# The mLSTM stage of a hybrid decoder step: its small work cut into five phases per pair of heads, and placed between the dense units by a written order

## The chip, the cores and the metric

The kernel runs on one core of one Trainium2 chip. Its time is the device time of one execution in microseconds (us). The core has five engines that each work through their own queue in order: TensorE (PE, matmuls; PEld is its loading of weights), VectorE (DVE), ScalarE (ACT), GpSimd (POOL), and SyncE (SP), which here only issues DMAs.

## The reference

One inference step of a two-layer trunk, on 512 prompt columns and 32 sample columns (8 sequences of 4). Layer 1's mixer, the mLSTM, is the part that changes:

```python
proj = xn @ w_in
qk_raw, v, o_pre, if_pre = jnp.split(proj, [...], axis=-1)
qk = conv_b + sum(conv_w[j] * xpad[:, j:j + T] for j in range(4))     # causal convolution
q, k = jnp.split(jax.nn.silu(qk), 2, axis=-1)                         # 8 heads of 64
o = jax.nn.sigmoid(o_pre)
def chunk_step(carry, inp):
    C, n, m = carry
    ...
    S = jnp.einsum('bhtk,bhsk->bhts', q_c, k_c) * Dw
    num = w_inter[..., None] * jnp.einsum('bhvk,bhtk->bhtv', C, q_c) + jnp.einsum('bhts,bhsv->bhtv', S, v_c)
    den = w_inter * jnp.einsum('bhk,bhtk->bht', n, q_c) + S.sum(-1)
    h = num / jnp.maximum(jnp.abs(den), jnp.exp(-m_t))[..., None]
    C = w_state[..., None, None] * C + jnp.einsum('bhs,bhsv,bhsk->bhvk', w_s, v_c, k_c)
    ...
h = h * lax.rsqrt(jnp.mean(h * h, -1, keepdims=True) + NORM_EPS) * norm_w
out = (h * o) @ w_out
```

## The kernel before

Activations lie with features on the 128 partitions and the 544 columns (512 prompt, 32 sample) along the free axis. `PARTS` cuts the columns into 256 and 288. Every dense product is fp32 made of three fp32r matmuls (`mm3`: high by high, high by low, low by high), so each weight tile that a DMA on SP brings (`wr`) is first split, ACT writing the high half (`wh`, in `split`) and DVE the low half (`wl`). A dense product of 8 blocks over one part is 24 matmuls into one PSUM bank (tag `ps`); with two banks in this stage, the third such unit may begin when DVE has read the first one out.

The stage (`mlstm`) first projects gates and values (`mlstm_inputs`), then in the scope `ml2`: 16 units of 24 matmuls for q and k (`mlstm_qk`, four pairs of heads j, each with a q block and a k block; DVE multiplies each part by the norm factor into `raw`, and then does the causal convolution in nine steps), 16 units of 24 for the output gates (`mlstm_gate`, tag `og`), and 32 units of 12 for the output projection (`project_out`, two halves of four heads, DVE adding each into `x`): 384 matmuls each. After it follows the feed-forward `f1b`.

The small work of a pair is fp32 matmuls of at most 129 columns. `mlstm_weights` loads two rows by DMA and spreads them over the partitions (`qi` from `dwi`, `d` from `dc`), makes the decay weights `d` on DVE and ACT, and multiplies them by k times q (L1376, L1381). `mlstm_pair` then goes chunk by chunk (z = 0 to 3 of 128 columns, z = 4 the samples): transpose k (L1404) and scale it on ACT into `kt`, weights times values (L1413), `qi` times the state (L1415), copy to `hx` and sum of squares on ACT, the next state (L1445 and DVE's L1448, L1450); for the samples also L1426, and L1438 with DVE's update of `cn`. `mlstm_heads` normalises `hx` (ACT's square root, DVE's L1475) and transposes it back (L1479). `mlstm_out` multiplies by the gate and splits for the output projection.

What stands in which order is decided by the Tile scheduler, from the order in the program and its own estimate of times; `high_priority(MOFF)` draws the small work ahead of program order:

```python
for j in range(4):
    if j < 3:
        self.mlstm_qk(j + 1, xs, rs)
    with self.tc.high_priority(MOFF):
        if j < 3:
            self.mlstm_weights(j + 1)
        self.mlstm_pair(j)
        self.mlstm_heads(j)
```

Of the kernel before, what the change touches and what calls it, by code (L numbers as in the profile page):

```python
# [13 lines left out]
ALU = mybir.AluOpType  # L14
# [17 lines left out]
NOG = 6  # L32
# [3 lines left out]
MOFF = 1000  # L36
# [205 lines left out]

class Trunk:
# [255 lines left out]
    def project_out(self, name, xs, halves=1):  # L499

        n = KT // halves
        for ks in (range(h * n, (h + 1) * n) for h in range(halves)):
            xk = [xs(k) for k in ks]
            for m in range(KT):
                def evac(i, hs, ps, m=m):
                    self.V.tensor_tensor(self.x[m][:, hs], ps, self.x[m][:, hs], op=ALU.add)
                self.dense(self.a[name][m][:, ks.start * P:ks.stop * P], xk, evac)
# [641 lines left out]
    def mlstm(self):  # L1149
        with self.scope("ml", nps=0):  # L1150
# [11 lines left out]
            with self.scope("ml2", nps=2):  # L1162
                self.wS, self.hx = {}, {}
                self.mlstm_qk(0, xs, rs)
                with self.tc.high_priority(MOFF):
                    self.mlstm_weights(0)
                for j in range(4):
                    if j < 3:
                        self.mlstm_qk(j + 1, xs, rs)
                    with self.tc.high_priority(MOFF):  # L1170
                        if j < 3:
                            self.mlstm_weights(j + 1)
                        self.mlstm_pair(j)
                        self.mlstm_heads(j)
                ogs = [self.mlstm_gate(h, xs, rs) for h in range(NOG)]
                ys = [self.mlstm_out(h, ogs[h]) for h in range(8 - NOG)]
                ogs += [self.mlstm_gate(h, xs, rs) for h in range(NOG, 8)]
                self.project_out("m_out", lambda h: ys[h] if h < len(ys) else self.mlstm_out(h, ogs[h]), 2)

    def mlstm_inputs(self, xs, rs):  # L1180
# [29 lines left out]
        for g in range(2):  # L1210
# [12 lines left out]
            if g == 0:  # L1223
# [78 lines left out]
    def mlstm_qk(self, j, xs, rs):  # L1302

        V, S, seq, cvo = self.V, self.S, self.by_seq, self.cvo
        cv0v = self.cv0.rearrange("p (k b t) -> p k b t", k=8, t=3)
        for mt in (j, 4 + j):
            raw = self.unit("raw", 2)

            def evac(i, hs, ps, raw=raw):
                V.tensor_tensor(raw[:, hs], ps, rs[i], op=ALU.mult)  # L1310
            self.dense(self.a["m_qk"][mt], xs, evac)
# [13 lines left out]
            (self.q if mt < 4 else self.k)[j] = acc  # L1325
        if j == 3:
            self.nc.sync.dma_start(self.o["o_conv"], cvo)

    def mlstm_gate(self, h, xs, rs):
        t = self.rp("og", NOG, [P, TT])  # L1330

        def evac(i, hs, ps):
            self.V.tensor_tensor(t[:, hs], ps, rs[i], op=ALU.mult)
        self.dense(self.a["m_o"][h], xs, evac)
        self.S.activation(t, t, AF.Tanh, scale=0.5)
        self.V.tensor_scalar(t, t, 0.5, 0.5, op0=ALU.mult, op1=ALU.add)
        return t
# [8 lines left out]
    def mlstm_weights(self, j):  # L1346
# [5 lines left out]
        pS_ = lambda: self.bank("pS", 2)  # L1352
# [4 lines left out]
        wl = self.local("wl_", 2, [P, 4])  # L1357
# [159 lines left out]
```

## Time and profile before

| | |
|---|---|
| median of 3 runs | 2579.95 us (2577.47 to 2580.44) |
| the profiled execution | 2580.45 us |
| its span, first to last instruction | 2578.7 us |
| mean granted clock of TensorE | 0.966 |
| the mLSTM stage from its first q/k matmul to the first matmul of `f1b` | 1913.6 to 2163.4 us of the span |

Times in the views are us from the span's start. An fp32 matmul stands in the trace as two PE instructions, an fp32r one as one. A granted clock of 1.00 is 2.4 GHz, 0.50 is 1.2 GHz; a mean between them is a stretch that had both. "Idle before" an instruction is how long its engine had nothing, and the arrow names what ended that. Some matmul records are missing from the trace, a few per cent.

### The profile page before, as it was taken

Reading aid. Unit: us, or ns where it says so; the run is one execution under the profiler, and the core shown is the slowest. Engines: PE = TensorE matmul, PEld = TensorE weight load, DVE = VectorE, ACT = ScalarE, POOL = GpSimd, SP = SyncE. Lnnn points to the kernel's source line nnn. Section 1 sums busy time; section 2 is a strip of 40 time slices with the busy share of each in tenths; the row PEclk is TensorE's granted clock in tenths of the full one; section 3 lists DMA queues with packets and bytes.
Section 4 is the critical chain, followed back from the end, with each engine's and each line's share of the span. In section 5 each row is a group of like instructions: output and inputs, shape, how many; then the busy total and the mean of one; then the engine's idle time right before and its main releaser. Section 6 shows DMA issues by size and latency. Waiting matters only on the chain.

```text
span 2578.7 us, 54194 instructions
## 1 busy us (share of the span) xinstructions
PE 2476.4 (96%) x21731; PEld 2323.5 (90%) x21731; DVE 1583.1 (61%) x3178; ACT 1258.1 (49%) x2772; POOL 497.6 (19%) x514
## 2 busy tenths in 40 slices
PE   9998999999889999998999999999998999999997
PEld 8998988888778788897999999999977879999997
DVE  6668787777897786665666544433536546444433
ACT  6555666665666564564555433332435435333322
POOL 1204333233431342330110011110000000111100
PEclk9999999999789899998999999999998979999999
DMA  7564543324233233453555432233242212223232
GB/s 218 182 195 143 159 125 113 113 90 137 80 97 111 86 98 116 120 163 116 163 166 167 121 95 85 84 92 91 81 113 80 65 56 91 90 83 94 84 90 72
DMA packets 102220, 291.63 MB, mean 113 GB/s; under 512 B 12569, under 2 KB 28345, under 8 KB 101969
## 3 DMA queue, kind: packets, MB, share of 16 engines
q1 hardware_dynamic: 101968, 288.18, 36.8%
q8 instruction: 170, 2.79, 0.4%
q14 instruction: 82, 0.66, 0.1%
HBM read 278.76 MB, written 9.38 MB: 112 GB/s over the span
## 4 chain that ended last, share of the span: by engine, by line
PE 85%; DVE 9%; issue 2%; ACT 2%; DMA 1%; POOL 1%; SPq 0%; DVEq 0%; ACTq 0%; POOLq 0%
PE ps L346 17%; PE ps L348 17%; PE ps L347 17%; PE pd L346 7%; PE pd L347 7%; PE pd L348 7%; DVE wl L343 2%; DVE m L668 1%; PE ps L1220 1%; PE ps L1221 1%; PE ps L1222 1%; PE b L912 1%; PE ps L1110 1%; PE pc L1034 1%; DVE mx L670 1%
## 5 line engine op out<-in xcount | busy, mean ns | idle before, releaser
L343 DVE TENSOR_TENSOR wl<-wr,wh 128x512 fp32r<-128x512 f32 (+2 forms) x1025 | 723.8, 708 | 480.4 <-ACT wh L342 450.1
L342 ACT CAST wh<-wr 128x512 fp32r<-128x512 f32 (+2 forms) x1025 | 621.8, 609 | 672.8 <-PE ps L347 433.2
L346 PE MATMUL ps<-a,wh 128*128 128x288 f32 (+1 forms) x2384 | 698.5, 293 | 12.3 <-ACT a L394 5.1
L348 PE MATMUL ps<-a,wl 128*128 128x288 f32 (+1 forms) x2384 | 694.3, 291 | 0.2 <-DVE wl L343 0.2
L347 PE MATMUL ps<-a,wh 128*128 128x288 f32 (+1 forms) x2384 | 688.4, 289 | 0.3
L346 PEld LDWEIGHTS ps<-a,wh 128*128 128x128 f32 x2384 | 453.0, 190 | 16.3 <-ACT a L394 5.6
L347 PEld LDWEIGHTS ps<-a,wh 128*128 128x128 f32 x2384 | 453.0, 190 | 2.3 <-DVE a L395 1.1
L348 PEld LDWEIGHTS ps<-a,wl 128*128 128x128 f32 x2384 | 450.7, 189 | 1.4 <-DVE wl L343 0.4
L418 POOL TENSOR_TENSOR t<-t,t 128x256 f32<-128x256 f32 (+1 forms) x132 | 141.6, 1073 | 858.0 <-ACT wh L342 409.9
L346 PE MATMUL ps<-h,wh 128*128 128x288 f32 (+1 forms) x1056 | 303.9, 288 | 0.0
L347 PE MATMUL ps<-h,wh 128*128 128x288 f32 (+1 forms) x1056 | 303.4, 287 | 0.0
L348 PE MATMUL ps<-h,wl 128*128 128x288 f32 (+1 forms) x1056 | 303.2, 287 | 0.0
L346 PE MATMUL pd<-rk,wh 128*128 128x288 f32 (+1 forms) x656 | 198.2, 303 | 6.4 <-DVE t L478 2.7
L347 PE MATMUL pd<-rk,wh 128*128 128x288 f32 (+1 forms) x656 | 197.9, 302 | 1.1 <-DVE rk L395 1.1
L348 PEld LDWEIGHTS ps<-h,wl 128*128 128x128 f32 x1056 | 198.9, 188 | 0.0
L347 PEld LDWEIGHTS ps<-h,wh 128*128 128x128 f32 x1056 | 198.9, 188 | 0.0
L346 PEld LDWEIGHTS ps<-h,wh 128*128 128x128 f32 x1056 | 198.6, 188 | 0.0
L348 PE MATMUL pd<-rk,wl 128*128 128x288 f32 (+1 forms) x656 | 196.7, 300 | 0.0
L342 ACT CAST h<-t 128x256 fp32r<-128x256 f32 (+1 forms) x132 | 55.3, 419 | 198.4 <-POOL t L418 198.4
L347 PE MATMUL pd<-mx,wh 128*128 128x256 f32 (+1 forms) x448 | 135.5, 304 | 9.5 <-DVE mx L670 6.6
L346 PE MATMUL pd<-mx,wh 128*128 128x256 f32 (+1 forms) x448 | 134.0, 302 | 4.2 <-ACT rk L691 1.9
L346 PEld LDWEIGHTS pd<-rk,wh 128*128 128x128 f32 x656 | 127.2, 194 | 10.0 <-ACT mx L669 2.9
(451 smaller groups left out, 4586.2 us busy)
## 6 DMA issues: line engine op xcount, KB each, us to landing
wr<-in_f0a_u_dram SPq DMA_DIRECT2D x44, 512.0 KB, 3.7
wr<-in_f0b_g_dram SPq DMA_DIRECT2D x44, 512.0 KB, 3.6
wr<-in_f0b_u_dram SPq DMA_DIRECT2D x44, 512.0 KB, 3.5
wr<-in_f0a_g_dram SPq DMA_DIRECT2D x43, 512.0 KB, 3.6
wr<-in_f0b_d_dram SPq DMA_DIRECT2D x24, 512.0 KB, 3.7
wr<-in_f1a_g_dram SPq DMA_DIRECT2D x22, 512.0 KB, 4.7
wr<-in_f1a_u_dram SPq DMA_DIRECT2D x22, 512.0 KB, 3.5
wr<-in_f1b_g_dram SPq DMA_DIRECT2D x22, 512.0 KB, 3.6
```

Source lines behind the costliest of these rows:

```text
L342: self.S.copy(dst_h, src)
L343: self.V.tensor_tensor(dst_l, src, dst_h, op=ALU.subtract)
L346: self.T.matmul(out, wh, xh, start=start, stop=False)
L347: self.T.matmul(out, wh, xl, start=False, stop=False)
L348: self.T.matmul(out, wl, xh, start=False, stop=stop)
L418: self.G.tensor_tensor(s, s, w, op=ALU.mult)
L668: V.scalar_tensor_tensor(m, d, self.vec("mu", c * 8 + k), xn, op0=ALU.mult, op1=ALU.add)
L670: (self.G if k % 2 else V).tensor_tensor(l, m, h.bitcast(F32), op=ALU.subtract)
L912: T.matmul(pg[:, (1 - h) * 512 + i * P:(1 - h) * 512 + (i + 1) * P], flat(xc[R[h], i]), flat(arc[R[h], i]), start=True, stop=True)
L1034: T.matmul(py[R[h], out(a)], uv[:, a, c, h, :], gm[:, a, c, 1 - h, 64:128], start=True, stop=st is None)
L1110: T.matmul(pn[R[h], :], xt[H, h * 64:(h + 1) * 64], um, start=True, stop=True)
L1220: T.matmul(pss[q][:n, :], xs[k][0][:, ts], wt(cs)[0], start=k == 0, stop=False)
```

## The change

`dense`'s products of the stage become lists of units (one part of one block each: `dense_units`, `project_units`), in one list `todo`: the q and k blocks of pairs 1 to 3, the gates, then the output projection. Pair 0's q and k run ahead of it. The small work of a pair becomes five phases over all chunks (`mlstm_weights`, `mlstm_states`, `mlstm_values`, `mlstm_sample`, `mlstm_heads`), twenty in all, in one list `small`. A loop walks through `todo` and calls the next phase each time another twentieth of the cost written for the first 44 units (2 for each of 28, 1 for each of 16) is done; the last phases so fall among the units of the output projection's first half. No priority is set any more, and the scheduler orders the rest.

Inside the phases: k is transposed four chunks to a bank and scaled into `kt` by one DVE operation (before: two on ACT for each chunk); all states come before all values; `hx` is copied three chunks at a time and its squares are read from SBUF; the scaling of `hx` is one DVE operation for all chunks and both heads (before: ten); the transposed gate columns `cols` are copied at once. `qi` becomes one full tile of 128 partitions for each head, with the other head's half set to zero by POOL, and L1415's product over 64 rows becomes one over 128 (L1494). The PSUM banks `pS`, `px` and `po` (two each) become six of `sm`. `d` has four buffers in place of six, `qi` four (two pairs) in place of three (three pairs), `og` five in place of six.

```diff
-NOG = 6
+NOG = 5
...
+    def sm(self):
+        return self.bank("sm", 6)
...
+    def dense_units(self, ap, xs, evac):
+
+        wt = []
+
+        def unit(i, hs):
+            if not wt:
+                wt.append(self.weight(ap))
+            ps = self.ps()[:, :hs.stop - hs.start]
+            n = ap.shape[-1] // P
+            for k in range(n):
+                x = xs[k]
+                self.mm3(ps, *wt[0](slice(k * P, (k + 1) * P)), x[0][:, hs], x[1][:, hs], k == 0, k == n - 1)
+            evac(i, hs, ps)
+        return [lambda i=i, hs=hs: unit(i, hs) for i, hs in enumerate(PARTS)]
+
+    def project_units(self, name, ys, half):
+
+        units = []
+        for m in range(KT):
+            def evac(i, hs, ps, m=m):
+                self.V.tensor_tensor(self.x[m][:, hs], ps, self.x[m][:, hs], op=ALU.add)
+            ks = slice(half * 4 * P, (half + 1) * 4 * P)
+            units += self.dense_units(self.a[name][m][:, ks], Shift(ys, half * 4), evac)
+        return units
...
-                self.mlstm_qk(0, xs, rs)
-                with self.tc.high_priority(MOFF):
-                    self.mlstm_weights(0)
+                for u in self.mlstm_qk(0, xs, rs):
+                    u()
+
+                ogs, ys = {}, {}
+                todo = [u for j in range(1, 4) for u in self.mlstm_qk(j, xs, rs)]
+                for h in range(8):
+                    todo += self.mlstm_gate(h, xs, rs, ogs)
+                for half in range(2):
+                    todo += self.project_units("m_out", ys, half)
+                cost = [2] * 28 + [1] * 32
+                small = []
                 for j in range(4):
-                    if j < 3:
-                        self.mlstm_qk(j + 1, xs, rs)
-                    with self.tc.high_priority(MOFF):
-                        if j < 3:
-                            self.mlstm_weights(j + 1)
-                        self.mlstm_pair(j)
-                        self.mlstm_heads(j)
-                ogs = [self.mlstm_gate(h, xs, rs) for h in range(NOG)]
-                ys = [self.mlstm_out(h, ogs[h]) for h in range(8 - NOG)]
-                ogs += [self.mlstm_gate(h, xs, rs) for h in range(NOG, 8)]
-                self.project_out("m_out", lambda h: ys[h] if h < len(ys) else self.mlstm_out(h, ogs[h]), 2)
+                    small += [lambda j=j: self.mlstm_weights(j), lambda j=j: self.mlstm_states(j),
+                              lambda j=j: self.mlstm_values(j), lambda j=j: self.mlstm_sample(j),
+                              lambda j=j: self.mlstm_heads(j)]
+                done, per = 0, sum(cost[:44]) / len(small)
+                for i, u in enumerate(todo):
+                    while small and done >= per * (20 - len(small)):
+                        small.pop(0)()
+                    for h in range(8):
+                        if h in self.hn and h in ogs and h not in ys:
+                            ys[h] = self.mlstm_out(h, ogs[h])
+                    u()
+                    done += cost[i]
...
-        qi = self.unit("qi", 3)
-        for h in range(2):
-            nc.sync.dma_start(qi[R[h]], self.rows["wi"][2 * j + h:2 * j + h + 1, :].to_broadcast([64, TT]))
+
+        qi = [self.unit("qi", 4) for _ in range(2)]
         wl = self.local("wl_", 2, [P, 4])
-        S.copy(wl, qi[:, MLC - 1:TP:MLC])
-        V.tensor_tensor(qi, q, qi, op=ALU.mult)
-
-        wS = [self.unit("d", 6) for _ in range(2)]
+        for h in range(2):
+            self.G.memset(qi[h][R[1 - h]], 0.0)
+            nc.sync.dma_start(qi[h][R[h]], self.rows["wi"][2 * j + h:2 * j + h + 1, :].to_broadcast([64, TT]))
+            S.copy(wl[R[h]], qi[h][R[h], MLC - 1:TP:MLC])
+            V.tensor_tensor(qi[h][R[h]], q[R[h]], qi[h][R[h]], op=ALU.mult)
+
+        wS = [self.unit("d", 4) for _ in range(2)]
         for h, d in enumerate(wS):
             hd = 2 * j + h
             nc.sync.dma_start(d, self.rows["c"][hd:hd + 1, :].to_broadcast([P, TT]))
@@ -1369,95 +1416,129 @@
                                    self.csmask[0:TS], op0=ALU.add, op1=ALU.add)
             S.activation(d[:, :TP], d[:, :TP], AF.Exp)
             S.activation(d[0:TS, TP:], d[0:TS, TP:], AF.Exp)
-        pS = [pS_() for _ in range(2)]
+
+        kt = self.local("kt", 2, [P, 5, P])
+        px, pe = self.sm(), self.sm()
+        for z in range(4):
+            T.transpose(px[:, z * P:(z + 1) * P], k[:, z * MLC:(z + 1) * MLC], self.ident)
+        T.transpose(pe[:TS, :P], k[:, TP:], self.ident)
+        for p, zs, n in ((px, slice(0, 4), P), (pe[:, :P], slice(4, 5), TS)):
+            nz = zs.stop - zs.start
+            V.tensor_tensor(kt[:n, zs].rearrange("p z (h d) -> p z h d", h=2), p[:n].rearrange("p (z h d) -> p z h d", z=nz, h=2),
+                            cols[:n, zs, 8 + 2 * j:10 + 2 * j].unsqueeze(3).to_broadcast([n, nz, 2, 64]), op=ALU.mult)
+        pS = [self.sm() for _ in range(2)]
         for z in range(4):
             ts = slice(z * MLC, (z + 1) * MLC)
             for h in range(2):
                 T.matmul(pS[h][:, ts], k[R[h], ts], q[R[h], ts], start=True, stop=True)
+        pe = [self.sm() for _ in range(2)]
+        for h in range(2):
+            T.matmul(pe[h][:TS, :TS], k[R[h], TP:], q[R[h], TP:], start=True, stop=True)
         for h, d in enumerate(wS):
             V.tensor_tensor(d[:, :TP], d[:, :TP], pS[h], op=ALU.mult)
-        pS = [pS_() for _ in range(2)]
-        for h in range(2):
-            T.matmul(pS[h][:TS, :TS], k[R[h], TP:], q[R[h], TP:], start=True, stop=True)
-        for h, d in enumerate(wS):
-            V.tensor_tensor(d[0:TS, TP:], d[0:TS, TP:], pS[h][0:TS, :TS], op=ALU.mult)
-        self.wS[j] = wS, qi, wl
-
+            V.tensor_tensor(d[0:TS, TP:], d[0:TS, TP:], pe[h][0:TS, :TS], op=ALU.mult)
+        self.wS[j] = wS, qi, wl, kt
...
-    def mlstm_pair(self, j):
...
-        for z in range(5):
-            pk = px()
-            T.transpose(pk[:n, :P], k[:, ts], self.ident)
-                S.activation(kt[:n, h * 64:(h + 1) * 64], pk[:n, h * 64:(h + 1) * 64], AF.Copy, scale=cols[:n, z, 8 + hd:9 + hd])
-                po = po_()
-                T.matmul(po[:n, :129], wS[h][:n, ts], vt, start=True, stop=z == 0)
-                if z in (1, 2, 3):
-                    T.matmul(po[:n, :129], qi[R[h], ts], st[R[h], :], start=False, stop=True)
-                S.copy(hx[:n, z, h, :], po[:n, :129])
...
+    def mlstm_states(self, j):
...
+        pn = [self.sm() for _ in range(2)]
+        sts = []
+        for z in range(4):
+            p = pn[z // 3][:, z % 3 * 129:z % 3 * 129 + 129]
+            for h in range(2):
+                hd = 2 * j + h
+                T.matmul(p[R[h]], kt[:, z, h * 64:(h + 1) * 64], self.v1[z][hd // 4][:, hd % 4, :], start=True, stop=True)
+        for z in range(4):
+            p = pn[z // 3][:, z % 3 * 129:z % 3 * 129 + 129]
+            st = self.local("st", 5, [P, 129])
+            if z == 0:
+                V.tensor_copy(st, p)
+            else:
+                V.scalar_tensor_tensor(st, sts[-1], wl[:, z:z + 1], p, op0=ALU.mult, op1=ALU.add)
+            sts.append(st)
...
+    def mlstm_values(self, j):
...
+        pa, pb = [self.sm() for _ in range(2)], [self.sm() for _ in range(2)]
+        at = lambda h, z, n=P: (pa[h] if z < 3 else pb[h])[:n, z % 3 * 129:z % 3 * 129 + 129]
+        for h in range(2):
+            hd = 2 * j + h
+            for z in range(4):
+                ts = slice(z * MLC, (z + 1) * MLC)
+                T.matmul(at(h, z), wS[h][:, ts], self.v1[z][hd // 4][:, hd % 4, :], start=True, stop=z == 0)
+                if z:
+                    T.matmul(at(h, z), qi[h][:, ts], st[z - 1], start=False, stop=True)
...
+            S.copy(hx[:, 0:3, h, :], pa[h][:, :387].rearrange("p (z v) -> p z v", z=3))
+            S.copy(hx[:, 3, h, :], at(h, 3))
+            S.copy(hx[:TS, 4, h, :], at(h, 4, TS))
...
+                S.activation(sq[:n], hx[:n, z, h, :128], AF.Square, accum_out=sc[:n, z, h:h + 1])
...
+    def mlstm_sample(self, j):
...
     def mlstm_heads(self, j):
...
+        V.tensor_tensor(hx[:, :, :, :128], hx[:, :, :, :128], s(4).unsqueeze(3).to_broadcast([P, 5, 2, 128]), op=ALU.mult)
...
-                V.tensor_scalar(hx[:n, z, h, :128], hx[:n, z, h, :128], sc[:n, z, 8 + h:9 + h], None, op0=ALU.mult)
```

PE, pair 3 in the program before: its values (`po`) with the weights `d_26996` and `d_26997`, the state `st`, and the sample products `km`, with no dense product among them.

```order
L1413 MATMUL po_27237<-v_4407_25391,d_26996 128x129
L1413 MATMUL po_27242<-v_4407_25391,d_26997 128x129
L1413 MATMUL po_27257<-v_4409_25393,d_26996 128x129
L1415 MATMUL po_27257<-st_27250,qi_26990 128x129
L1413 MATMUL po_27263<-v_4409_25393,d_26997 128x129
L1415 MATMUL po_27263<-st_27250,qi_26990 128x129
L1438 MATMUL pS_27342<-v_4415_25399,km_27340 128x129
L1413 MATMUL po_27279<-v_4411_25395,d_26996 128x129
```

PE, pair 3 in the changed program: the same products (L1492 and L1494, into `sm`), between units of the output projection (`ps`, L356 to L358).

```order
L356 MATMUL ps_27737<-hi_27220,wh_27733 128x256
L357 MATMUL ps_27737<-k_27221,wh_27733 128x256
L358 MATMUL ps_27737<-hi_27220,wl_27734 128x256
L1494 MATMUL sm_27817<-st_27722,qi_27593 128x129
L1492 MATMUL sm_27817<-v_4411_25395,d_27604 128x129
L1494 MATMUL sm_27817<-st_27724,qi_27593 128x129
L1494 MATMUL sm_27819<-st_27726,qi_27593 128x129
L1492 MATMUL sm_27818<-v_4407_25391,d_27605 128x129
L356 MATMUL ps_27751<-hi_26879,wh_27733 128x288
```

Before, about 40 small products of pair 3 stood behind one another; now a unit of 12 dense matmuls stands between every few of them. In pairs 1 and 2 the phases are not cut: the 24 products of `mlstm_values` stand together there, with units of 24 ahead and behind.

DVE in the program before, while pair 0's sample states (`cn`) and norm factors (`sc`) are made: the decay weights of pair 3 (`d_26996`, `d_26997`) stand among them.

```order
L1463 TENSOR_TENSOR sc_26246<-sc_26246,cols_25388 128x5x2
L1367 SCALAR_TENSOR_TENSOR d_26996<-d_26996,cols_25388,c_c_ml_25211 128x128 x2
L1464 RECIPROCAL sc_26246<-sc_26246 128x5x2
L1367 SCALAR_TENSOR_TENSOR d_26996<-d_26996,cols_25388,c_c_ml_25211 128x128
L1439 SCALAR_TENSOR_TENSOR cn_26374<-cn_26374,ws_25841,pS_26390 128x129
L1367 SCALAR_TENSOR_TENSOR d_26996<-d_26996,cols_25388,c_c_ml_25211 128x128
L1368 SCALAR_TENSOR_TENSOR d_26996<-d_26996,cols_25388,c_c_ml_25211 32x32
```

DVE in the changed program, at the same work of pair 0: here it is the decay weights of pair 2 (`d_27084`, `d_27085`), and the read-out of a q/k unit (`raw_26438`) stands behind them.

```order
L1534 SCALAR_TENSOR_TENSOR cn_26231<-cn_26231,ws_25831,sm_26381 128x129 x3
L1414 SCALAR_TENSOR_TENSOR d_27084<-d_27084,cols_25388,c_c_ml_25211 128x128
L1534 SCALAR_TENSOR_TENSOR cn_26231<-cn_26231,ws_25831,sm_26382 128x129
L1414 SCALAR_TENSOR_TENSOR d_27084<-d_27084,cols_25388,c_c_ml_25211 128x128 x3
L1415 SCALAR_TENSOR_TENSOR d_27084<-d_27084,cols_25388,c_c_ml_25211 32x32
L1534 SCALAR_TENSOR_TENSOR cn_26238<-cn_26238,ws_25831,sm_26387 128x129 x3
L1414 SCALAR_TENSOR_TENSOR d_27085<-d_27085,cols_25388,c_c_ml_25211 128x128
L1534 SCALAR_TENSOR_TENSOR cn_26238<-cn_26238,ws_25831,sm_26388 128x129
L1414 SCALAR_TENSOR_TENSOR d_27085<-d_27085,cols_25388,c_c_ml_25211 128x128
L1368 TENSOR_SCALAR q_26364<-q_26364 128x544
L1414 SCALAR_TENSOR_TENSOR d_27085<-d_27085,cols_25388,c_c_ml_25211 128x128 x2
```

With four buffers of `d`, pair 2 takes pair 0's, so the DMA that fills them can start only behind pair 0's values; before, with six, that held for pair 3 alone.

## Rows read from the trace of the kernel before

**Rows 1.** The page's head: span, and the engines' busy time, share of it and instructions.
```profile
span 2578.7 us, 54194 instructions
PE 2476.4 (96%) x21731; PEld 2323.5 (90%) x21731; DVE 1583.1 (61%) x3178; ACT 1258.1 (49%) x2772; POOL 497.6 (19%) x514
```

**Rows 2.** Stretches: length, busy us (instructions) of each engine, granted clock, DMA share, GB/s.
```profile
1940.00:1950.00 10.00, 10.00 (x87) 9.75 (x87) 10.00 (x27) 6.45 (x18) 0.00 (x0) 1.00 0.31 107
1690.00:1755.00 65.00, 65.00 (x520) 65.00 (x519) 23.91 (x44) 19.71 (x38) 4.31 (x5) 1.00 0.31 89
1913.60:1923.00 9.40, 7.79 (x48) 7.56 (x48) 2.78 (x12) 0.94 (x3) 0.00 (x0) 0.82 0.89 229
1923.00:1977.00 54.00, 53.18 (x408) 48.42 (x409) 37.75 (x106) 29.91 (x98) 2.03 (x2) 0.97 0.35 102
1977.00:1998.00 21.00, 12.09 (x51) 9.74 (x50) 14.67 (x57) 12.09 (x31) 0.00 (x0) 0.55 0.24 78
1998.00:2083.00 85.00, 84.22 (x625) 73.90 (x624) 46.60 (x125) 42.82 (x127) 4.63 (x4) 0.99 0.21 63
2083.00:2112.50 29.50, 27.51 (x104) 18.47 (x104) 12.33 (x48) 10.35 (x47) 2.49 (x2) 0.53 0.18 56
2112.50:2163.40 50.90, 49.80 (x383) 49.33 (x382) 37.10 (x77) 22.07 (x46) 0.00 (x0) 0.97 0.28 89
1913.60:2163.40 249.80, 234.59 (x1612) 207.43 (x1612) 151.24 (x420) 118.17 (x350) 9.16 (x8) 0.88 0.28 83
```

**Rows 3.** The chain, 1957 to 2040: start us, us, what (x instructions).
```profile
1957.29 1.09 PE pS L1376 x16
...
1961.61 0.17 PE pS L1381 x2
...
1965.64 0.37 PE pS L1445 x4
...
1968.18 0.42 PE po L1415 x4
...
1970.46 0.42 PE po L1413 x2
1970.88 0.42 PE po L1415 x2
1971.30 0.37 PE px L1404 x2
...
1972.30 0.64 PE pS L1438 x4
...
1974.95 4.28 DMA d<-dc
...
2023.76 1.00 PE po L1426 x8
...
2039.03 0.44 PE po L1479 x4
```

**Rows 4.** PE in order of time, 1980 to 1999, with its waits.
```profile
1980.51 1.47 PE L1438 MATMUL pS<-v,km 32*128 32x129 f32 x4 [2.18 <-DVE cn L1439]
1985.57 1.33 PE L1479 MATMUL po<-c_c_all,hx 128*128 128x128 f32 x5 [3.60 <-DVE hx L1475]
...
1993.54 0.58 PE L346 MATMUL ps<-a,wh 128*128 128x256 f32 x1 [1.77 <-DVE raw L1310]
...
1998.19 0.41 PE L346 MATMUL ps<-a,wh 128*128 128x256 f32 x1
```

**Rows 5.** The chain in the tail of pair 3, 2083 to 2112.
```profile
2095.60 0.73 PE po L1413 x2
...
2109.00 2.04 DVE hx L1475 x10
```

**Rows 6.** DVE in order of time, with its waits.
```profile
1979.25 0.61 DVE L1367 SCALAR_TENSOR_TENSOR d<-d,cols,c_c_ml 128x128 f32<-128x128 f32 x2 [1.40 <-DMA d<-dc]
```

**Rows 7.** SP's issues in order of time (the line's two DMAs together).
```profile
1913.35 1.15 SPq L1356 DMA_DIRECT2D qi<-dwi  x2
```

More of the change, by code (lines that the diff above doesn't have):

```diff
@@ L35 @@
 NW = 4
-MOFF = 1000
 FILL = {0: 4, 1: 4, 2: 1, 3: 4, 5: 3, 14: 3}
@@ L497, in ffn_units @@
         return us
[L499 to L507, printed above, removed]
+    def dense_units(self, ap, xs, evac):
[18 more added lines that the diff above has]
+        return units
     def final(self):
@@ L1305, in mlstm_qk, with evac, conv @@
         cv0v = self.cv0.rearrange("p (k b t) -> p k b t", k=8, t=3)
+        units = []
         for mt in (j, 4 + j):
[L1307 to L1311, printed above, removed]
+            raw = {}
+            def evac(i, hs, ps, raw=raw, mt=mt):
+                if i == 0:
+                    raw[0] = self.unit("raw", 2)
+                V.tensor_tensor(raw[0][:, hs], ps, rs[i], op=ALU.mult)
+                if i == 1:
+                    conv(mt, raw[0])
+            units += self.dense_units(self.a["m_qk"][mt], xs, evac)
+        def conv(mt, raw):
             S.copy(cvo[:, mt, 0:3], raw[:, TP - 3:TP])
@@ new lines, in mlstm_values @@
+        for h in range(2):
+            hd = 2 * j + h
+            T.matmul(at(h, 4, TS), wS[h][:TS, TP:], self.v1[4][hd // 4][:TS, hd % 4, :], start=True, stop=False)
+            for b4 in range(4):
+                T.matmul(at(h, 4, TS), qms[h][:, b4 * TS:(b4 + 1) * TS], cns[h][:, b4, :], start=False, stop=b4 == 3)
+        for h in range(2):
+            S.copy(hx[:, 0:3, h, :], pa[h][:, :387].rearrange("p (z v) -> p z v", z=3))
+            S.copy(hx[:, 3, h, :], at(h, 3))
+            S.copy(hx[:TS, 4, h, :], at(h, 4, TS))
+            for z in range(5):
+                n = P if z < 4 else TS
+                sq = self.local("sq", 2, [P, P])
+                S.activation(sq[:n], hx[:n, z, h, :128], AF.Square, accum_out=sc[:n, z, h:h + 1])
@@ new lines, in mlstm_values @@
+        self.hx[j] = hx, sc, cns
+    def mlstm_sample(self, j):
+        nc, V, G, T = self.nc, self.V, self.G, self.T
+        kt = self.wS[j][3]
+        kms = []
+        for h in range(2):
+            km = self.local("km", 2, [TS, 512])
+            G.tensor_tensor(km.rearrange("p (b d) -> p b d", b=NB),
+                            kt[:TS, 4, h * 64:(h + 1) * 64].unsqueeze(1).to_broadcast([TS, NB, 64]),
+                            self.seqm[:TS].unsqueeze(2).to_broadcast([TS, NB, 64]), op=ALU.mult)
+            kms.append(km)
+        pns = []
+        for h in range(2):
+            hd = 2 * j + h
+            pn = [self.sm() for _ in range(2)]
+            for b4 in range(4):
+                p = pn[b4 // 3][:, b4 % 3 * 129:b4 % 3 * 129 + 129]
+                T.matmul(p, kms[h][:, b4 * P:(b4 + 1) * P], self.v1[4][hd // 4][:TS, hd % 4, :], start=True, stop=True)
+            pns.append(pn)
+        for h in range(2):
+            hd = 2 * j + h
+            cn = self.hx[j][2][h]
+            for b4 in range(4):
+                p = pns[h][b4 // 3][:, b4 % 3 * 129:b4 % 3 * 129 + 129]
+                V.scalar_tensor_tensor(cn[:, b4, :], cn[:, b4, :], self.ws[:, hd * 4 + b4:hd * 4 + b4 + 1], p, op0=ALU.mult, op1=ALU.add)
+            nc.sync.dma_start(self.o["sCN"][hd], cn.rearrange("p b v -> p (b v)"))
```

118 lines of the change are left out of this document (48 added, 70 removed).

## The prediction

> **What bounds the kernel now.** I read the page's head first [rows 1]: PE is busy for 96% of the span, so the program is bound by PE almost everywhere, and 0.2% of it, 5.2 us, is about what a measurement of this kernel can tell from no change. The program's instructions are the same up to the inputs of the mLSTM stage and again behind it, so all that counts is in 1913.6 to 2163.4: 249.8 us, PE busy for 234.6 of them at a mean granted clock of 0.88 [rows 2]. A busy PE at half clock is half lost, so I cut the stage where the clock changes, and then priced the work in it.
>
> The work at full clock. Dense: 1152 matmuls at 65.00 / 520 = 0.125 us (the row of an undisturbed dense stretch, [rows 2]) are 144.0 us. Small, per pair, from pieces of the chain at full clock [rows 3]: L1376 1.09; L1381 2 x 0.17 = 0.34; L1404 5 x 0.185 = 0.92; L1445 4 x 0.37 = 1.48; L1413 eight at 0.42 and two of the samples at about 0.33 (my estimate), 4.02; L1415 6 x 0.42 = 2.52; L1426 2 x 1.00; L1438 4 x 0.64 = 2.56; L1479 four at 0.44 and a short one, twice, about 1.1. That is 16.0, and 64.0 for four pairs. Together 208.0, so 41.8 us are lost. Of these PE is idle for 249.8 - 234.6 = 15.2. What half clock costs is (1 - granted clock) x busy, by stretch [rows 2]: 1.40 + 1.60 + 5.44 + 0.84 + 12.93 + 1.49 = 23.7. The other 2.9 I put down to switches between small and dense products.
>
> Two stretches hold most of it. In 1977 to 1998 (lost 8.9 idle + 5.4 clock = 14.3) DVE waits 1.40 for the weights `d` of pair 3, which take 4.28 from issue to landing [rows 3, 6]; behind it stand pair 0's `cn`, `hx` and a `raw`, and PE waits 2.18, 3.60 and 1.77 for them in turn [rows 4]. The clock falls after the first of these waits and stays at 1.2 GHz for about 5 us after dense work has begun again at 1993.54: the matmul at 1998.19 still has 0.41 [rows 4]. In 2083 to 2112.5 (lost 2.0 + 12.9 = 14.9) no dense work is left that the scheduler could put between pair 3's chain, the clock is 0.53 [rows 2], and a product takes 0.73 where it took 0.42 [rows 3, 5]. Against this stands 1998 to 2083: small work mixed with dense ran there at 0.99, with 1.6 us lost in 85 [rows 2].
>
> **The change part by part.** PE's count of instructions does not change, so the 208.0 stays. What changes is the losses, stage by stage.
>
> *The tail of pair 3* now lies between units of the output projection, as the order on PE shows: 16.0 us of small among 16 units of 12 x 0.125 = 1.5 us, 24 us of dense. I take the row of 1998 to 2083, where small and dense were mixed in about such shares, and count all of the quiet stage, about 190 us, at its rate: 1.6 x 190 / 85 = 3.6 us. This replaces the 14.9 of the tail, the 2.4 of 1923 to 1977 (0.8 idle, 1.6 clock) and the 1.6 of 1998 to 2083. The 2.6 of the last stretch (1.1 idle, 1.5 clock) keeps its idle 1.1; the clock's part was the recovery from the tail and goes.
>
> *The wait on `d`.* It is not removed but moves a pair earlier: with four buffers, pair 2's `d` may be loaded only when pair 0's values are done, and by DVE's order pair 2's decay weights stand among pair 0's `cn`, with a q/k unit's `raw` behind them. From the end of pair 0's values: issue of `qi` ahead on SP 1.15 [rows 7], landing 4.28 [rows 3], then on DVE eight operations at about 0.29, two short ones, five `cn` and a `raw`, about 4.8 at the 0.61 for two of [rows 6]: 10.2 us. PE has until then the sample products, 4 x 0.64 = 2.56, and 34 matmuls of the units begun, 34 x 0.125 = 4.25: 6.8. It waits 3.4. As the clock fell after a wait of 2.18 [rows 4], I add its recovery, 5 us as in those rows at 0.55 [rows 2], 2.2 lost: 5.6 in place of 14.3. Bounds: nil, if the load's issue comes early, and 14.3 as before. Pair 3's `d` waits likewise for pair 1's values, with more units to cover it: 1.0, between nil and 5.6.
>
> *The start* lost 1.6 + 1.4 = 3.0 [rows 2]. SP's queue now has two loads of `cn` (128 x 516, 0.26 MB each) ahead of pair 1's `d`, and the second unit's `raw` stands behind that `d` on DVE: at 229 GB/s [rows 2] the loads are 2.3 us, part of which the first units cover. I take 1.5 more, 4.5, between 3.0 and 5.3.
>
> *`qi` over 128 rows.* Three pairs of L1415 products stood back to back on the two halves of the rows, and such four instructions took 0.42, no more than two (the x4 and the x2 of L1415 in [rows 3]; the other such pieces are at 2011.5 and 2063.9). With full rows that is gone: 3 x 0.42 = 1.3, between nil and 1.3. The Trainium skill (TensorE: Matmul & The Clock Gate, "Part 3: Packing small matmuls — row/col tiling") speaks against this edit more strongly: products on distinct row groups run at the same time, which would save half of all 24 products. By it 12 x 0.42 = 5.0 would be lost, 3.7 more than by the rows, and the sum would come out near 2563. The rows show the sharing only where two such products were neighbours with no wait between them.
>
> *DVE* loses operations (`kt` in one, L1475's ten in one, 2.04 before [rows 5]) and gains `kt` from ACT and a second `qi` product for each pair; ten of its ten us were busy in 1940 to 1950 while PE was too [rows 2]. Its work in the stage, 151 of 250 us, stays within about 4 us by my estimate. I add 1.0 for waits where it is late, between nil and the rival below. ACT at 118 of 250 has room and loses work; POOL's eight memsets are off every wait, since POOL works 9 us in the stage [rows 2]. The switches stay, 2.9.
>
> Sum of losses after: 4.5 + 3.6 + 5.6 + 1.0 + 1.1 + 1.3 + 1.0 + 2.9 = 21.0, against 41.8: 20.8 gained. From the profiled execution, 2580.45 (1.75 more than its span), that leaves 2559.6; its time is 0.5 above the median, so I forecast 2559.
>
> **The rivals.**
> - *The new waits do not show.* Start 3.0, quiet 2.3, end 1.1, switches 1.9: 8.3 lost, 33.5 gained, 2546. For it speaks that the stage's DVE had room after 1998; against it that the order on DVE puts a `raw` behind `d`. Chance 0.12.
> - *The values blocks run at half clock.* In pairs 1 and 2 the phase is not cut: 4.02 + 2.52 + 2.00 = 8.5 us of small products in a piece. If the clock falls halfway, 4.2 of its work takes twice as long, and 2.2 more go in the recovery: 12.8 for two, and 2572. Wholly at half clock it would be 2 x (8.5 + 2.2) = 21.4, and 2580. Against it: 1969.97 to 1976.6 was mostly uninterrupted small work in a stretch at 0.97 [rows 2]. Chance 0.18, at 2567 to 2576.
> - *The spreading gives nothing.* DVE becomes the bound in the 12 q/k units that now carry pair 0's and 1's phases: from 10 of 10 [rows 2] an overrun of 1.6 us for each unit of 3 us eats 20 us, 2580. It needs half a unit more of DVE's work than before. Chance 0.08.
> - *Slower.* In pair 3's phases the units are of 12, 1.5 us each, too short to bring the clock back, as 5 us of dense did not at 1993.54 [rows 4]. If all 40 us of that stage run at the 0.53 of [rows 2], they take 75: 35 more, 2594. It ends above the time before from 30 us of such work on (30 x 0.47 / 0.53 = 26.6). Against it: 1998 to 2083 at 0.99. Chance 0.07.
>
> **How the numbers follow.** The forecast case, 2550 to 2567 by its terms' bounds, has 0.55. The range takes it, the fewer waits (to 2545) and the values blocks (to 2576), about 0.83 with the tails cut. Faster by over 0.2%: the first three, 0.85; within 0.2% 0.08; slower 0.07.
>
> **What would show it.** Right: `f1b` begins near 2143; PE's idle time in the stage is about 10 us, half of it at two places, the start and a `raw` read-out behind a DMA of `d` during pair 0's samples; no stretch at a clock under 0.6 longer than 7 us; pair 3's products back at 0.42. Wrong: a clock near 0.5 in a values block or among the output projection's units; PE waiting for `raw` in every q/k unit; the products by `qi` costing more than 0.42 each. The forecast fails most easily on the clock, which I have only from mixtures that another order made.

## The result, and the profile after

The changed kernel takes 2537.52 us (median of four, 2533.85 to 2541.78) against 2580.19 (2577.47 to 2582.65): ratio 0.9835, interval 0.9817 to 0.9854. It is 42.7 us faster where 21 were forecast, and lies below the range. The profiled execution, 2541.78, is the longest of the four. Single executions differ by some 5 us in the stages ahead of the mLSTM too, so kernels are compared below by their medians and by the length of the stage in the trace, from its first q/k matmul to the first of `f1b`: 249.9 us before, 210.8 after, 207.8 in a second profile of the changed kernel.

The page's head after, for [rows 1]:

```profile
span 2539.8 us, 54086 instructions
PE 2445.1 (96%) x21731; PEld 2310.1 (91%) x21731; DVE 1587.1 (62%) x3154; ACT 1250.3 (49%) x2716; POOL 501.6 (20%) x522
```

The same number of matmuls keeps PE busy for 31 us less. The stretches of the stage (columns as in [rows 2]), cut where PE waits or the clock changes:

```profile
1913.81:1918.00 4.19, 4.19 (x22) 4.19 (x23) 0.51 (x3) 0.20 (x1) 2.02 (x4) 0.59 0.80 210
1918.00:1928.20 10.20, 6.70 (x53) 6.27 (x51) 5.32 (x19) 3.65 (x11) 0.00 (x0) 1.00 0.62 181
1928.20:1935.00 6.80, 6.80 (x42) 6.80 (x42) 6.53 (x19) 4.30 (x10) 0.00 (x0) 0.75 0.23 81
1935.00:1965.00 30.00, 30.00 (x257) 28.26 (x256) 26.35 (x71) 16.81 (x56) 3.51 (x4) 1.00 0.34 101
1965.00:1972.00 7.00, 5.76 (x46) 5.54 (x45) 6.86 (x23) 5.52 (x17) 0.00 (x0) 1.00 0.38 117
1972.00:2010.00 38.00, 37.52 (x311) 34.99 (x311) 30.91 (x89) 25.43 (x71) 3.50 (x4) 1.00 0.30 90
2010.00:2018.00 8.00, 5.97 (x34) 5.16 (x34) 7.08 (x15) 3.67 (x8) 0.00 (x0) 0.79 0.62 199
2018.00:2124.63 106.63, 105.90 (x862) 100.61 (x861) 72.25 (x161) 51.77 (x133) 4.61 (x4) 1.00 0.26 81
1913.81:2124.63 210.82, 202.84 (x1612) 191.82 (x1613) 155.82 (x396) 111.35 (x300) 13.65 (x16) 0.98 0.32 99
```

From 2018 on, pairs 2 and 3 and the output projection lose 0.7 us in 107, at full clock: the tail of [rows 2] is gone. Idle time is 8.0 us and half clock costs 0.41 x 4.19 + 0.25 x 6.80 + 0.21 x 5.97 = 4.7. PE's waits (in order of time, 1923 to 2013) are where they are left:

```profile
1923.14 0.39 PE L356 MATMUL ps<-a,wh 128*128 128x256 f32 x1 [1.55 <-DVE raw L1350]
1928.20 0.61 PE L356 MATMUL ps<-a,wh 128*128 128x288 f32 x1 [1.95 <-DVE raw L1350]
...
1969.69 0.39 PE L356 MATMUL ps<-a,wh 128*128 128x256 f32 x1 [1.24 <-DVE raw L1350]
...
2012.62 2.03 PE L1560 MATMUL sm<-c_c_all,hx 128*128 128x128 f32 x10 [2.03 <-DVE hx L1551]
```

What was not forecast is seen in pair 2's values on PE (the same view; the times of one row run past the start of the next, so a product's price is the distance of two starts):

```profile
2036.18 0.39 PE L1494 MATMUL sm<-st,qi 128*128 128x129 f32 x2
2036.40 0.39 PE L1492 MATMUL sm<-v,d 128*128 128x129 f32 x2
2036.63 0.39 PE L1494 MATMUL sm<-st,qi 128*128 128x129 f32 x2
2036.85 0.39 PE L1492 MATMUL sm<-v,d 128*128 128x129 f32 x2
...
2046.28 2.05 PE L1527 MATMUL sm<-v,km 32*128 32x129 f32 x16
```

A product (two instructions) starts 0.22 us behind the one before, where the rows of [rows 3] have 0.42, at full clock in both; eight sample products take 2.05 where four pieces of 0.64 took 2.56. So the small work itself became cheaper. The table adds these distances over the stage, each counted for the product that it starts from, idle time taken off (so half clock is in them), by kind of work; "in" is the experiment or kernel, "values" are the products by `d`, "states" the sample products by `km`. "Half clock" is the part of dense and small that the clock cost, each distance times (1 - granted clock) by the clock's own steps in the trace (for the change 5.1, where the stretches above gave 4.7). "Work" is what dense and small are without it, at full clock. "Changes" counts the instructions that use another part of the array than the one ahead: in a row, `64*128` is that part, rows times columns.

| in | median | stage | dense | values | by qi | states | all small | idle | half clock | work | changes |
|---|---|---|---|---|---|---|---|---|---|---|---|
| before | 2580.19 | 249.9 | 160.6 | 16.6 | 10.6 | 14.7 | 74.1 | 15.2 | 24.1 | 210.6 | 148 |
| b_order | 2556.46 | 227.6 | 158.8 | 13.8 | 8.9 | 11.7 | 64.1 | 4.8 | 5.0 | 217.9 | 171 |
| b_order128 | 2552.79 | 223.0 | 159.2 | 10.3 | 5.4 | 12.5 | 57.0 | 6.8 | 3.4 | 212.8 | 142 |
| the change | 2537.52 | 210.8 | 153.3 | 9.3 | 5.6 | 8.1 | 49.5 | 8.0 | 5.1 | 197.7 | 70 |
| the change again | 2537.03 | 207.8 | 152.5 | 9.3 | 5.6 | 8.1 | 48.7 | 6.6 | 3.4 | 197.8 | 70 |
| q64 | 2539.97 | 210.3 | 153.1 | 11.4 | 8.2 | 8.1 | 53.1 | 4.1 | 3.4 | 202.8 | 104 |
| q64pair | 2536.64 | 205.5 | 152.0 | 10.1 | 5.3 | 8.1 | 48.9 | 4.6 | 1.7 | 199.2 | 90 |
| b_ctl | 2580.03 | 249.6 | 159.6 | 17.3 | 10.6 | 14.5 | 75.1 | 14.9 | 24.5 | 210.2 | 145 |
| b128 | 2571.38 | 238.6 | 159.6 | 13.3 | 6.0 | 12.5 | 61.9 | 17.1 | 15.5 | 206.0 | 107 |

In the three kernels with the old order, before, b_ctl and b128, "work" is too small by an estimated 1 to 2 us: a product with its change took 0.73 at half clock [rows 5] for 0.42 at full [rows 3], less than twice as long.

### The profile page after: what moved, and what is told of

Read it like the earlier page. It is cut to its first block, busy times and chain, and to the rows that moved or that the text cites. A ratio compares the mean times of both kernels' runs of the same rounds, so it can differ in the third digit from the quotient of the medians.

```text
span 2539.8 us, 54086 instructions
## 1 busy us (share of the span) xinstructions
PE 2445.1 (96%) x21731; PEld 2310.1 (91%) x21731; DVE 1587.1 (62%) x3154; ACT 1250.3 (49%) x2716; POOL 501.6 (20%) x522
## 4 chain that ended last, share of the span: by engine, by line
PE 84%; DVE 9%; issue 2%; ACT 2%; DMA 1%; POOL 1%; SPq 0%; DVEq 0%; ACTq 0%; POOLq 0%
PE ps L356 17%; PE ps L358 17%; PE ps L357 17%; PE pd L356 7%; PE pd L357 7%; PE pd L358 7%; DVE wl L353 2%; DVE m L693 1%; PE ps L1254 1%; PE ps L1256 1%; PE ps L1255 1%; PE b L937 1%; PE ps L1135 1%; DVE mx L695 1%; PE pc L1059 1%
## 5 line engine op out<-in xcount | busy, mean ns | idle before, releaser
L356 PE MATMUL ps<-a,wh 128*128 128x288 f32 (+1 forms) x2384 | 698.0, 293 | 13.5 <-ACT a L404 5.0
L358 PE MATMUL ps<-a,wl 128*128 128x288 f32 (+1 forms) x2384 | 692.6, 291 | 0.0
L356 PEld LDWEIGHTS ps<-a,wh 128*128 128x128 f32 x2384 | 452.8, 190 | 16.9 <-DVE raw L1350 5.4
L358 PEld LDWEIGHTS ps<-a,wl 128*128 128x128 f32 x2384 | 450.0, 189 | 0.5 <-DVE wl L353 0.2
L356 PE MATMUL ps<-h,wh 128*128 128x288 f32 (+1 forms) x1056 | 303.9, 288 | 0.0
L358 PE MATMUL ps<-h,wl 128*128 128x288 f32 (+1 forms) x1056 | 303.2, 287 | 0.0
L356 PE MATMUL pd<-rk,wh 128*128 128x288 f32 (+1 forms) x656 | 199.0, 304 | 6.8 <-DVE t L488 2.9
L358 PEld LDWEIGHTS ps<-h,wl 128*128 128x128 f32 x1056 | 198.9, 188 | 0.0
L356 PEld LDWEIGHTS ps<-h,wh 128*128 128x128 f32 x1056 | 198.6, 188 | 0.0
L358 PE MATMUL pd<-rk,wl 128*128 128x288 f32 (+1 forms) x656 | 197.2, 301 | 0.0
L356 PE MATMUL pd<-mx,wh 128*128 128x256 f32 (+1 forms) x448 | 133.8, 302 | 4.3 <-ACT rk L716 1.9
L356 PEld LDWEIGHTS pd<-rk,wh 128*128 128x128 f32 x656 | 128.0, 195 | 10.5 <-ACT mx L694 2.9
```

The source lines that it names most:

```text
L356: self.T.matmul(out, wh, xh, start=start, stop=False)
L358: self.T.matmul(out, wl, xh, start=False, stop=stop)
```

## The experiments

The theory after the result: TensorE takes about 0.2 us more for a product over other rows of the array than the one ahead of it (128, 64, 32), and 0.1 for a dense matmul behind a small one; the phases and the full `qi` remove such places. The rival is the prediction's reading of the rows, by which only the heads' sharing of the array counts. The kernel as changed ran again beside the first three:

> The changed kernel once more, as the measure for the three kernels beside it: 2538, between 2534 and 2542.

It took 2537.03 (2534.42 to 2540.49).

**q64: `qi` over 64 rows again.**

```diff
-        qi = [self.unit("qi", 4) for _ in range(2)]
+        qi = self.unit("qi", 2)
...
-                    T.matmul(at(h, z), qi[h][:, ts], st[z - 1], start=False, stop=True)
+                    T.matmul(at(h, z), qi[R[h], ts], st[z - 1][R[h], :], start=False, stop=True)
```

> The changed kernel with qi again one tile per pair, so that its products are over 64 rows; all else stays. Theory (a product over other rows than the one ahead of it costs 0.2 us more, 0.42 in place of 0.22): 32 such places come back (8 behind dense, 11 behind a value product, 13 value products behind one by qi), 6.4 us, less 5 pairs of heads that share the array, 1.1: about 5 slower than the changed kernel, 2543. Rival (the prediction's term: only the shared pairs count): 0 to 1.3 faster than the changed kernel, 2537 to 2538.

2539.97, 2.9 slower than the changed kernel beside it, with ranges that overlap a little (from 2539.53 here, to 2540.49 there), so that the rows have to decide. Its pair 2 on PE:

```profile
2029.72 0.49 PE L1493 MATMUL sm<-st,qi 64*128 64x129 f32 x2
2030.13 0.49 PE L1491 MATMUL sm<-v,d 128*128 128x129 f32 x2
2030.55 0.49 PE L1493 MATMUL sm<-st,qi 64*128 64x129 f32 x2
2030.97 0.71 PE L1491 MATMUL sm<-v,d 128*128 128x129 f32 x4
```

Each product behind one over other rows takes 0.42, the full ones too; the second of the two full ones in the last row adds only 0.22. Values and products by `qi` take 4.7 us more (table), as the theory has it, and the work at full clock is 5.0 more; 2 to 4 us of it came back as less idle time. The waits that are gone are those at 1969 and 2012; that it is because DVE and ACT do one `qi` for two is likely, but was not shown. The rival has the wrong sign.

**q64pair: the same 64 rows, in runs of their kind.**

```diff
+        for f, zs in ((vm, (0, 1, 3)), (qm_, (1, 3)), (vm, (2,)), (qm_, (2,))):
+            for z in zs:
+                for h in range(2):
+                    f(h, z)
```

Here `vm` is the value product of q64 and `qm_` its product by `qi`.

> As q64, but the value products and the products by qi written in runs of their kind, the two heads' qi products side by side. Theory (the change of rows costs, not the product over 64 rows): 16 places are left, 3.2 us, and 12 shared pairs give back 2.6: within 1.5 of the changed kernel, 2538. Rival (a product over 64 rows costs 0.42 wherever it stands): 24 x 0.2 = 4.8 slower, 2543, like q64.

2536.64, 0.4 faster than the changed kernel: the theory. On PE:

```profile
2029.75 1.50 PE L1487 MATMUL sm<-v,d 128*128 128x129 f32 x12
2031.18 0.72 PE L1488 MATMUL sm<-st,qi 64*128 64x129 f32 x8
2031.83 0.71 PE L1487 MATMUL sm<-v,d 128*128 128x129 f32 x4
2032.47 0.49 PE L1488 MATMUL sm<-st,qi 64*128 64x129 f32 x4
2032.89 0.40 PE L1495 MATMUL sm<-v,d 32*32 32x129 f32 x2
```

Four products over 64 rows take 0.65, two take 0.42: 0.2 for the change and then 0.22 for each pair of heads. So they do share the array, and both readings of the x4 in [rows 3] meet: it had a change of rows and a shared pair.

**What counts as a change.** The theory names rows alone, and a price of 0.1 for a dense matmul behind a small one. The trace of the changed kernel, at full clock, corrects both:

```profile
1949.68 0.28 PE L357 MATMUL ps<-a,wh 128*128 128x256 f32 x1
1949.89 1.10 PE L1453 MATMUL sm<-v,kt 128*64 128x129 f32 x16
1950.92 0.39 PE L358 MATMUL ps<-a,wl 128*128 128x256 f32 x1
1951.14 0.61 PE L1492 MATMUL sm<-v,d 128*128 128x129 f32 x4
1951.51 0.38 PE L356 MATMUL ps<-a,wh 128*128 128x288 f32 x1
1951.72 0.29 PE L357 MATMUL ps<-a,wh 128*128 128x288 f32 x1
```

The products by `kt` use all 128 rows, but 64 columns. The dense matmul ahead of them takes 0.21 and the one behind them 0.22, both in place of 0.125: columns cost as rows do. The values use the whole array, as dense work does. The dense matmul behind them takes 0.21 too, but the two products themselves took 0.37 in place of 0.45, so nothing is lost there. The 0.1 is thus one half of the price of a change, the other half of which lies on the instruction ahead, and no price of its own.

**b_ctl and b128: the full `qi` alone, in the kernel before.** b128 makes `qi` as the changed kernel does; b_ctl has five `d` and two `qi` and is else the kernel before. The order on PE is nearly the same in both: by the traces it differs among pair 0's units and at one place among the products by `kt` and `hx`, which the expectation below did not foresee.

```diff
-        qi = self.unit("qi", 3)
+        qi = [self.unit("qi", 4) for _ in range(2)]
...
+            self.G.memset(qi[h][R[1 - h]], 0.0)
...
-        wS = [self.unit("d", 6) for _ in range(2)]
+        wS = [self.unit("d", 5) for _ in range(2)]
...
-                    T.matmul(po[:n, :129], qi[R[h], ts], st[R[h], :], start=False, stop=True)
+                    T.matmul(po[:n, :129], qi[h][:, ts], st, start=False, stop=True)
```

> The kernel before with two buffers of qi and five of d, the control for the kernel beside it. A wait for d or qi may come earlier: 2578 to 2588.

> The control with qi as two full tiles of 128 rows, the other head's half zero; PE's order is the control's. Theory (a change of rows costs 0.2): 29 places fewer (18 products by qi behind a value product, 8 the other way, 3 behind dense), 5.8 at full clock and up to 7 where the clock is half, less 0.7 for the three shared pairs: 5 to 6 faster than the control. Rival (the prediction's term): 0.7 to 1.3 slower than the control. By the Trainium skill's rule on row groups (TensorE: Matmul & The Clock Gate, Part 3): up to 5 slower.

2580.03 and 2571.38: 8.7 faster by the full rows alone, 11.0 in the stage. The sign is the theory's. That it is more than 5 to 6 is the clock: of the 11.0, work at full clock is 4.2 and half clock 9.0, and idle time takes 2.2 back (table). The tail's granted clock was 0.50 in b_ctl (2083 to 2116) and 0.69 in b128 (2080 to 2107); why it fell less there was not tested. The theory's 29 places are 38 by the traces, since it left out some behind the products by `qi`. The Trainium skill's rule on row groups (TensorE: Matmul & The Clock Gate, Part 3), that such products run at the same time, spoke against this edit; q64pair agrees with it for a run of such products (four in 0.65), and in b_ctl's order the changes outweigh it.

**b_order: the written order alone.** The changed kernel's loop and units, with the old small work, four `d`, two `qi` and five `og`:

```diff
-                    small += [lambda j=j: self.mlstm_weights(j), lambda j=j: self.mlstm_states(j),
-                              lambda j=j: self.mlstm_values(j), lambda j=j: self.mlstm_sample(j),
-                              lambda j=j: self.mlstm_heads(j)]
+                    small += [lambda j=j: self.mlstm_weights(j), lambda j=j: self.mlstm_pair(j), lambda j=j: self.mlstm_heads(j)]
```

> The changed kernel's loop and list of units, with the small work of the kernel before: weights, the pair chunk by chunk, heads; three phases per pair, products by qi over 64 rows, the banks pS, px and po, four d and two qi. Theory (the written order alone gives what the prediction counted: the tail's 14.9 and most of the wait's 14.3 go, 0.2 for each change of rows stays): 18 to 24 faster than before, 2555 to 2561. Rival (only the phases make work that can be spread; chunk by chunk the chain is as long as before): under 10 faster, 2570 or more.

2556.46, 23.3 faster than the 2579.79 beside it. The stretches that were lost before:

```profile
1977.00:1998.00 21.00, 19.85 (x127) 15.28 (x126) 16.73 (x53) 11.99 (x41) 2.04 (x2) 0.84 0.25 80
1998.00:2083.00 85.00, 85.00 (x616) 74.60 (x616) 51.09 (x138) 44.02 (x124) 2.48 (x2) 1.00 0.26 80
2083.00:2112.00 29.00, 29.00 (x208) 25.11 (x208) 15.71 (x46) 11.32 (x39) 2.04 (x2) 1.00 0.21 67
```

Chunk by chunk, the chain spreads as well as in phases, and the clock stays up. Its small work is 64.1 us (table), but with half clock in it; its work at full clock is 7.3 above that of the kernel before, with 23 more changes, and its gain is all in idle time and half clock, 39.3 before and 9.8 here.

**b_order128: with the full `qi`.** To b_order's `mlstm_weights` and `mlstm_pair` the edit of b128, with four `d` as in b_order.

> As b_order, with qi as two full tiles of 128 rows as in the changed kernel. Theory: 25 places where the rows change go, 5.0, and four shared pairs, 0.9: 4 to 7 faster than b_order, and what then is left to the changed kernel, some 12 to 16, is the grouping in phases. Rival (phases matter only by the rows of qi): it comes within 3 of the changed kernel, 2541 or less.

2552.79: 3.7 faster than b_order, 4.6 in the stage. The 15.3 that remain to the changed kernel are the phases, with all that is done otherwise inside them. Of the stage's 12.2, 7.5 are small work and 5.9 dense, and idle time takes 1.2 back. The sample states show how (b_order128 on PE):

```profile
2017.65 0.48 PE L1484 MATMUL pS<-v,km 32*128 32x129 f32 x2
2018.07 0.39 PE L358 MATMUL ps<-a,wl 128*128 128x256 f32 x1
...
2018.65 0.48 PE L1484 MATMUL pS<-v,km 32*128 32x129 f32 x2
```

One product stands between dense matmuls at a time and pays the change each time; in the phase eight stand together. By the traces a dense matmul stands directly behind a small one at 71 places here and at 27 in the changed kernel, and there are 72 changes more here. The work at full clock is 15.1 more, 0.21 for each change. The same sum gives 0.21 between b_order and b_order128, 0.18 between the change and q64, and 0.20 between the change and q64pair, when the shared pairs (four, five and twelve at 0.22) are counted in. So the changes account for nearly the whole of what the phases took from PE's work.

**tail3: pair 3's phases called late.**

```diff
-                    while small and done >= per * (20 - len(small)):
+                    while small and (done >= per * (20 - len(small)) if len(small) > 5 else i >= 44):
```

> The changed kernel with pair 3's five phases called only behind the first half of the output projection, so that they stand together with no dense unit left to put between them, as before the change. Theory (the spreading gives what the prediction said, by the clock and by covered waits): about 12 us of small work run mostly at 1.2 GHz, 8 to 12 lost, and 2 to 6 of idle between the phases: 10 to 18 slower than the changed kernel, 2548 to 2556. Rival (with products in runs of one shape the tail no longer matters): 0 to 4 slower.

2545.75, 8.7 slower than the changed kernel, between the two. It does not decide: the scheduler still put dense units between the late phases, and the clock did not fall:

```profile
2080.00:2088.00 8.00, 8.00 (x65) 7.48 (x64) 2.19 (x5) 3.20 (x10) 0.00 (x0) 1.00 0.20 66
2088.00:2096.00 8.00, 8.00 (x61) 6.81 (x61) 3.50 (x9) 3.63 (x20) 0.00 (x0) 1.00 0.22 69
2096.00:2104.00 8.00, 7.22 (x54) 6.51 (x53) 5.92 (x17) 3.37 (x6) 0.00 (x0) 1.00 0.26 99
```

PE's waits for `raw` at the stage's start, 3.1 and 0.9 us, are little more than the changed kernel's 1.55 and 1.95. The stage is 8.5 longer than in the changed kernel's second profile: 4.3 idle (2.4 in place of 1.2 at pair 2's `d`, and 1.9 and 0.8 in front of `hx` in place of 1.3), 1.5 half clock and 2.7 work, with 9 changes more.

**pair_q4 and pair_q3d6: more buffers on q64pair.** pair_q4 has the first edit, pair_q3d6 the second:

```diff
-        qi = self.unit("qi", 2)
+        qi = self.unit("qi", 4)
...
-NOG = 5
+NOG = 4
-        qi = self.unit("qi", 2)
+        qi = self.unit("qi", 3)
-        wS = [self.unit("d", 4) for _ in range(2)]
+        wS = [self.unit("d", 6) for _ in range(2)]
```

> As q64pair, with a buffer of qi for each of the four pairs. Theory (ACT waits for the load of pair 3's qi, and hx and the transposes behind it are late: 2.0 idle and 1.7 of clock at 2012): that loss goes, 2 to 4 faster than q64pair. Rival (DVE, not ACT, is late there): no difference of more than 1.

> As q64pair, with six buffers of d, three of qi and four of og. Theory (two waits of the changed kernel hang on buffers: DVE's for pair 2's d, 1.2 idle on PE at 1969, and ACT's for pair 3's qi, 3.7 at 2012): 2 to 5 faster than the changed kernel, 2533 to 2536. Rival (loads that start earlier only make the start later, where 3.5 idle and 3.4 of clock are lost): 0 to 4 slower.

2540.24, 3.6 slower than q64pair, where both theories had none or a gain; and 2538.52, 1.9 slower than q64pair and 1.5 than the changed kernel, though run beside other kernels. In q64pair itself the wait for `hx` of 2012 had gone with the single `qi`, so buffers had nothing to win there. In both kernels the second wait for `raw` at the start is longer, 2.7 and 2.4 against 1.5: the rival of pair_q3d6. The stage is 2.2 and 2.1 longer than q64pair's, by 1.0 and 1.1 idle and 1.5 and 1.7 half clock. The rest of pair_q4's 3.6 lies outside the stage and stays open.

**poola and poold: `d` made on POOL.** In the changed kernel and in q64pair, so that no `raw` stands behind a wait for `d` on DVE:

```diff
-                V.scalar_tensor_tensor(d[:, zs], d[:, zs], cols[:, z, hd:hd + 1], self.cmask, op0=ALU.add, op1=ALU.add)
+            self.G.tensor_tensor(dz, dz, cols[:, 0:4, hd:hd + 1].to_broadcast([P, 4, MLC]), op=ALU.add)
+            self.G.tensor_tensor(dz, dz, self.cmask.unsqueeze(1).to_broadcast([P, 4, MLC]), op=ALU.add)
```

> The changed kernel with the two additions that make d moved from DVE to POOL, so that no read-out of a q/k unit stands behind a wait for d. Theory (the start's waits of 1.6 and 2.0 with 1.7 of clock, and the 1.2 at 1969, are d's): 4 to 6 faster than the changed kernel, 2531 to 2534. Rival (POOL takes some 8 us for a pair's d by its 1.07 for 256 columns, and pair 2's and 3's weights are late instead): no faster, 2537 or more.

> As poola, on q64pair (products by qi over 64 rows in runs of their kind). Theory: 4 to 6 faster than q64pair, 2530 to 2533. Rival as for poola: 2536 or more.

2547.86 and 2544.41, 10.8 and 7.8 slower. The rival has the sign, but not the mechanism: PE waits 7.9 us for `raw` at 1931, because of one DVE instruction of poola (DVE's and then POOL's in order of time):

```profile
1924.93 5.07 DVE L353 TENSOR_TENSOR wl<-wr,wh 128x512 fp32r<-128x512 f32 x1 [6.36 <-ACT wh L352]
```

```profile
1924.36 1.04 POOL L1413 TENSOR_TENSOR d<-d,cols 128x512 f32<-128x512 f32 x1
...
1928.19 1.25 POOL L1414 TENSOR_TENSOR d<-d,c_c_ml 128x512 f32<-128x512 f32 x1
1929.41 0.69 POOL L1416 TENSOR_TENSOR d<-d,c_c_ml 32x32 f32<-32x32 f32 x1
```

An operation of 0.67 us (the next of its kind, at 1933) stands for 5.07, about until POOL's additions end; in poold it stands for 5.64, again about until they end. And DVE came to it only after 6.36 idle: ACT, which makes `wh`, stood behind its own wait for `qi`, 5.7 us.

No kernel here beats the changed one by more than can be told: q64pair is level with it.

## Why the prediction was wrong

- **The step that failed** is "PE's count of instructions does not change, so the 208.0 stays". The count stayed, but PE's work at full clock fell from 210.6 (the prediction's 208.0 and the 2.9 that it put down to switches) to 197.7: 12.9 of the stage's 39.1, where the prediction had 1.3 the other way. The other 26.2 are idle time and half clock, 39.3 before and 13.1 after; there the prediction had 22.1, from 38.9 to 16.8, so its mechanism held and it was 4 short. What fell in the work are changes, 148 to 70. The pieces of [rows 3] were read rightly, but 0.42 was not a product's price: it was 0.22 and a change of rows. The same rows had L1376's sixteen instructions at 1.09, 0.14 a product; prices that differ so by neighbour were there to be seen.
- **`qi` over 128 rows** was sized 1.3 the wrong way: at full clock it gives 4.2 in the old order (b128) and 5.1 in the new one (b_order128), and undoing it costs 5.0 (q64). The row x4 in 0.42 was read as sharing alone.
- **The switches** were held at 2.9 and called unchanged; dense matmuls directly behind small ones fell from 55 to 27, and their cost lay in the 0.42s as well.
- **The sum** was right for the order alone, 208.0 + 21.0 = 229.0 forecast for the stage and 227.6 measured in b_order, but by luck. Its idle time and half clock are 9.8, where the terms for them had 16.8, and its work is 217.9, where the sum had 210.9: two misses of 7 that cancel. That the tail's 14.9 and most of the wait's 14.3 go was right.
- **The new waits** came where forecast. At the start they cost more than 4.5: waits of 1.55 and 1.95 and 3.4 of clock. At pair 2's `d` they cost less than 5.6: DVE waits 1.36 for the load, PE 1.24, and the clock stays. At 2012 `hx` is late by 2.0 with 1.3 of clock, against 1.0. That last wait goes with ACT's wait for the load of pair 3's `qi`, which stands ahead of `hx` on ACT: 2.67 and 2.03 in the first profile, 1.51 and 1.29 in the second. No experiment took it away alone.
- **The rivals**: the values blocks ran at full clock (2034 to 2040 lies in the stretch at 1.00). DVE did not become the bound, and pair 3's phases did not lower the clock. "The new waits do not show" was nearest in time and wrong in kind.

## What to carry to other kernels

Before summing small matmuls from a trace, price each kind by its neighbours: the distance of two starts within a run of one shape, and across a change. Where the two differ, order the work in runs of one shape, or give the products one shape, even at the price of multiplying zeros. A written order recovers waits and the clock; grouping by kind recovers content that no wait shows, since PE is busy in it.

## What the runs showed of the hardware

A change in the rows that a product uses costs about 0.2 us (0.42 against 0.22 in q64), whichever way it goes, half of it on the instruction ahead; so does a change in the columns (`kt` in the changed kernel, where the dense matmuls on both sides take 0.21 and 0.22 in place of 0.125). Within a run, two heads' products over 64 rows take 0.22 together (q64pair). A dense matmul behind a small product that uses the whole array costs nothing more. And a DVE operation that reads two operands stood for 5.07 us in place of 0.67 while POOL's additions ran (poola), and for 5.64 in poold; that it waited for them is read from the times alone.
